# Re-spaced side work in a two-layer sequence model: scan scalings, last chunks, first loads, and attention ordered as values, queries, pool input, outputs

## The chip, the cores and the metric

One core of a Trainium2 chip runs the whole program. Times are device microseconds from one execution of the program. The engines are TensorE (PE), VectorE (DVE), ScalarE (ACT), GpSimd (POOL) and SyncE (SP), which here only issues DMAs. A smaller time is better.

## The reference

A sequence of 256 tokens with 1024 features goes through two blocks.

The first block has two layers. In each layer:

```
u = rmsnorm(h) * norm_mix_g
z, xbc, dt, g_q, g_f, g_i, g_g, m_q, m_k, m_v, m_i, m_f, m_o, gates = split(u @ w_in)
merged = gate0*(ssd(z, xbc, dt) @ w_br_ssd) + gate1*(hgrn2(...) @ w_br_hg) + gate2*(mlstm(...) @ w_br_ml)
h = h + merged @ w_out
h = h + (silu(a) * v) @ w_down      # a, v: a depthwise convolution of rmsnorm(h) @ w_up
h = h + (p @ w_ple) * sigmoid(h @ w_ple_gate)
```

The branch `ssd` ends with a root-mean-square norm over two groups of 512 channels. The second block has one layer, where mod is a linear map of silu(c), cut into six vectors:

```
h = rms_norm(x) * (1 + sc1) + sh1
q, k, v, u = split(h @ w_in)             # 4 heads, 2 maps of 64 each, values of 128; u: 4 pool groups
a_out = softmax(q0 k0) v - lam * softmax(q1 k1) v, then rms_norm per head (rotary on q and k)
p_out = (windowed means of u, minus u) @ w_pool * pool_scale
x = x + g1 * (concat(a_out, p_out) @ w_out)
x = x + g2 * moe(rms_norm(x) * (1 + sc2) + sh2)     # 32 experts, top 2 in one group
```

All arithmetic is in fp32.

## The kernel before

Features lie on the partitions in 8 chunks of 128, and the 256 tokens on the free axis. A fp32 product is three matmuls on fp32r halves (`mm3`, L484 to L486, 256 columns each): hi by hi, hi by lo and lo by hi. A weight matrix comes in units of 128x1024, in the order of a plan. For each unit SP issues the load to `w_raw` (L257), ACT casts it to `w_hi` (L296), and DVE subtracts to `w_lo` (L308), up to three units ahead of PE. `s_proj` runs one projection: two output chunks of 128 share a PSUM tile, and each takes a unit of 8 blocks, that is 24 matmuls. The first pair of a projection with `first=True` interleaves the two units (L501 to L503), so that it can follow its input chunk by chunk. `m_proj` (L528 to L530) has the weights as the moving operand, with 512 columns.

Everything else runs between these matmuls. After certain blocks of a unit (`self.hooks`, positions 2 and 6 as a rule, 3, 6 and 8 in the wide projections) PE's program calls `hook()`, which moves the next generator of `bgs` or `par` by one `yield`. A plain `yield` ends the hook, and `yield True` lets the next generator run in it too. Since each engine executes its program in the order in which it was written, a PE instruction written at a hook holds every later matmul until its input is there. `defer` and `chain` put off single functions to later hooks in the same way.

The places that the change touches are these.

- The start: `h` and four units are loaded, ACT and DVE split `h` times the first gain (`raw_add`, L703, L704) for the first projection `z0`, the squares are summed by PE (`sum_sq`, L639, a matmul with a column of ones), `rstd` (L648, L649) and `wide` (L654) give the scale for all partitions, and `norm` (L716, L719, L712) forms the normalised chunks. The matmul for the attention's lambda (L606) waits for a short chain of VectorE and ScalarE work.
- The scan's end: `ssd` sums squares of its 8 channel chunks (L639, after an add L644 on DVE), takes `rstd` and `wide`, and scales chunk by chunk (L1190, L1193, L1195). Meanwhile the hgrn2 generator does its first passes (L1262 on PE, L1242 to L1293 on ACT and DVE).
- The last chunks of `brm`, `wout` and `down`: chunks 6 and 7 leave in one pair, and their squares are summed at the end.
- The second block: eight chunks of u (L1635 on DVE, L1614 on ACT, L1615 on DVE) feed the projections u2, v2, q2 and o2. Each head is a generator `attention`: rotary matmul (L1722), scores (L1736), exponentials (L1745), transposes (L1760), product with the values (L1768), and for two groups of heads (0 to 2, and 3) a norm and transposes (L1791). `pool` is another generator (L1837). o2 (L1704 to L1706) adds eight input chunks, the pool's first, and drains the generators in while loops.
- After o2 comes the MoE, whose 192 loads of 1 MB SP issues at L275.

Of the kernel before, what the change touches and what calls it, by code (L numbers as in the profile page):

```python
# [172 lines left out]
def layout(i):  # L173
# [194 lines left out]
class Net:  # L368
    def __init__(self, ctx, tc, aps, dbg=None):
# [19 lines left out]
        for n, a, b in (("u2", 0, 4), ("v2", 4, 8), ("q2", 8, 16), ("o2", 16, 24)):  # L389
            plan += [(n, aps["win2"][u], UW) for u in range(a, b)]  # L390
# [153 lines left out]
    def setup(self):  # L544
        nc, aps, cp = self.nc, self.aps, self.cp
        self.h = self.act.tile([128, 8, T], F32, name="h")
        self.vl = {}
        self.load_vec(0)
        for c in range(0, 8, 4):
            nc.sync.dma_start(self.h[:, c:c + 4], aps["xT"][:, c:c + 4])  # L550
            self.st.load()
# [16 lines left out]
        for c in range(0, 8, 2):  # L568
            self.raw_add(0, c)
            if c < 4:  # L570
                self.st.begin()
                self.st.end()
        self.st.fill()
# [4 lines left out]
        self.flush(once=True)  # L578

    def setup2(self, lv):  # L580
# [42 lines left out]
        self.chain(lambda: None, start, lam, end)  # L623
# [9 lines left out]
    def sum_sq(self, ps, sq, first, last, add=True):  # L633

        def mm():
            for j in range(1 if add else 2):
                for tt in range(2):
                    o = j * T + tt * 128
                    self.nc.tensor.matmul(ps[:, tt:tt + 1], sq[:, o:o + 128], self.one[:, 0:1],  # L639
                                          start=first and not j and not tt, stop=last and (add or j == 1),  # L640
                                          skip_group_check=True)
        if not add:
# [1644 lines left out]
```

## Time and profile before

| | before |
|---|---|
| time, median of 3 runs (lowest to highest) | 2145.73 us (2142.51 to 2146.99) |
| profiled execution: time, span | 2140.42 us, 2138.6 us |
| mean granted TensorE clock | 0.989 |
| PE busy | 2077.2 us (97%) |
| weight load (PEld) busy | 1749.9 us (82%) |
| DVE busy | 1358.7 us (64%) |
| ACT busy | 1053.4 us (49%) |
| matmul records of L484 to L486 | 3 x 3264 |
| mean of a weight cast (ACT, L296), of a low half (DVE, L308) | 1048 ns, 1215 ns |
| mean DMA rate over the span | 224 GB/s |

Busy PE time is modelled from the matmuls' starts, so a busy PE need not run at its full rate: what a stretch could take is better read from the distance of matmul starts. Idle time of an engine that nothing waits for costs nothing.

### The profile page before, as it was taken

Reading aid. Unit: us, or ns where it says so; the run is one execution under the profiler, and the core shown is the slowest. Engines: PE = TensorE matmul, PEld = TensorE weight load, DVE = VectorE, ACT = ScalarE, POOL = GpSimd, SP = SyncE. Lnnn points to the kernel's source line nnn. Section 1 sums busy time; section 2 is a strip of 40 time slices with the busy share of each in tenths; the row PEclk is TensorE's granted clock in tenths of the full one; section 3 lists DMA queues with packets and bytes.
Section 4 is the critical chain, followed back from the end, with each engine's and each line's share of the span. In section 5 each row is a group of like instructions: output and inputs, shape, how many; then the busy total and the mean of one; then the engine's idle time right before and its main releaser. Section 6 shows DMA issues by size and latency. Waiting matters only on the chain.

```text
span 2138.6 us, 37221 instructions
## 1 busy us (share of the span) xinstructions
PE 2077.2 (97%) x15222; PEld 1749.9 (82%) x15222; DVE 1358.7 (64%) x2399; ACT 1053.4 (49%) x1686; POOL 4.2 (0%) x10
## 2 busy tenths in 40 slices
PE   8999999999999999999999999999988999999987
PEld 8988999999999999799999999999978544444323
DVE  7897787775888778887777767887676210011002
ACT  6665665664666356666666745664444211111102
POOL 0000000000000000000000000000000000000000
PEclk9999999999999999999999999999999999999999
DMA  6433444445655844344343456558545999999996
GB/s 224 151 129 128 139 148 149 141 155 174 226 194 199 312 163 175 117 138 158 138 159 119 139 202 212 183 197 307 192 138 217 394 420 420 420 420 420 421 420 261
DMA packets 106095, 482.22 MB, mean 225 GB/s; under 512 B 11712, under 2 KB 13376, under 8 KB 81344
## 3 DMA queue, kind: packets, MB, share of 16 engines
q1 hardware_dynamic: 97024, 451.41, 56.6%
q10 hardware_dynamic: 8896, 28.37, 3.8%
q8 instruction: 122, 2.00, 0.4%
q14 instruction: 53, 0.43, 0.1%
HBM read 478.69 MB, written 1.05 MB: 224 GB/s over the span
## 4 chain that ended last, share of the span: by engine, by line
PE 71%; DMA 16%; DVE 6%; ACT 5%; issue 1%; ACTq 0%; SPq 0%; DVEq 0%
PE ps_d L484 16%; PE ps_d L485 16%; PE ps_d L486 15%; DMA s<-in_moe 7%; DMA w_more<-in_moe 7%; PE ps_d L2029 3%; PE ps_b L1262 2%; PE ps_d L528 2%; PE ps_d L530 2%; PE ps_d L529 2%; PE ps_d L2055 1%; DVE w_lo L308 1%; PE ps_d L502 1%; ACT w_hi L296 1%; PE ps_b L1146 1%
## 5 line engine op out<-in xcount | busy, mean ns | idle before, releaser
L484 PE MATMUL ps_d<-s,w_hi 128*128 128x256 f32 x3264 | 934.1, 286 | 0.0
L485 PE MATMUL ps_d<-s,w_hi 128*128 128x256 f32 x3264 | 915.2, 280 | 0.0
L486 PE MATMUL ps_d<-s,w_lo 128*128 128x256 f32 x3264 | 914.9, 280 | 0.0
L296 ACT CAST w_hi<-w_raw 128x1024 fp32r<-128x1024 f32 x474 | 490.5, 1048 | 291.6 <-PE ps_d L485 209.0
L484 PEld LDWEIGHTS ps_d<-s,w_hi 128*128 128x128 f32 x3264 | 617.5, 189 | 6.6 <-issue 5.8
L485 PEld LDWEIGHTS ps_d<-s,w_hi 128*128 128x128 f32 x3264 | 617.3, 189 | 1.1 <-issue 0.5
L486 PEld LDWEIGHTS ps_d<-s,w_lo 128*128 128x128 f32 x3264 | 616.5, 189 | 0.2
L308 DVE TENSOR_TENSOR w_lo<-w_raw,w_hi 128x1024 fp32r<-128x1024 f32 x474 | 569.6, 1215 | 46.4 <-ACT w_hi L296 46.4
L2037 DVE TENSOR_TENSOR x2a<-x2a,ps_d 128x512 f32<-128x512 f32 x16 | 11.0, 688 | 177.5 <-PE ps_d L2029 177.5
L2068 DVE SCALAR_TENSOR_TENSOR s<-ps_d,m_ws,s 128x512 fp32r<-128x512 f32 (+1 forms) x34 | 24.5, 720 | 145.1 <-ACT s L2067 145.1
L2029 PE MATMUL ps_d<-s,s 128*64 128x512 f32 x424 | 98.8, 599 | 1.1 <-DMA s<-in_moe 0.9
L893 DVE SCALAR_TENSOR_TENSOR x2a<-ps_d,vl,x2a 128x255 f32<-128x255 f32 x176 | 81.0, 481 | 27.2 <-ACT x2a L886 24.1
L2029 PE MATMUL ps_d<-w_more,s 128*64 128x512 f32 x384 | 90.5, 600 | 1.8 <-DMA w_more<-in_moe 1.7
L2067 ACT ACTIVATE s<-ps_d,m_ws 128x512 fp32r<-128x512 f32 (+1 forms) x34 | 22.6, 666 | 114.1 <-PE ps_d L2055 113.0
L1262 PE MATMUL ps_b<-s,s 128*128 128x128 f32 x512 | 71.2, 284 | 5.4 <-ACT s L1284 3.5
L1262 PEld LDWEIGHTS ps_b<-s,s 128*128 128x128 f32 x512 | 65.2, 191 | 7.0 <-ACT s L1284 4.3
L2029 PEld LDWEIGHTS ps_d<-s,s 128*64 128x64 f32 x424 | 27.7, 136 | 51.6 <-issue 40.9
L1284 ACT COPY s<-s 128x512 f32<-128x512 f32 x48 | 30.5, 636 | 73.5 <-DVE s L1280 73.4
L1536 DVE SCALAR_TENSOR_TENSOR s<-s,ada_c,s 128x1024 f32<-128x1024 f32 x42 | 53.8, 1282 | 18.6 <-DMA s<-in_wada 18.4
L2029 PEld LDWEIGHTS ps_d<-w_more,s 128*64 128x64 f32 x384 | 24.8, 136 | 48.5 <-issue 37.2
L2034 ACT ACTIVATE x2a<-ps_d 128x512 f32<-128x512 f32 x16 | 9.6, 600 | 106.0 <-PE ps_d L2029 106.0
L2055 PE MATMUL ps_d<-s,x2b 128*64 128x512 f32 x248 | 57.3, 599 | 3.9 <-DMA s<-in_moe 3.9
(419 smaller groups left out, 2757.3 us busy)
## 6 DMA issues: line engine op xcount, KB each, us to landing
w_raw<-in_wl SPq DMA_DIRECT2D x448, 512.0 KB, 4.4
s<-in_moe SPq DMA_DIRECT2D x84, 1024.0 KB, 19.8
w_more<-in_moe SPq DMA_DIRECT2D x72, 1024.0 KB, 19.8
w_raw<-in_moe SPq DMA_DIRECT2D x36, 1024.0 KB, 19.9
s<-in_wada ACTq DMA_DIRECT2D x48, 512.0 KB, 5.7
w_raw<-in_win SPq DMA_DIRECT2D x24, 512.0 KB, 4.5
h<-in_xT SPq DMA_DIRECT2D x2, 512.0 KB, 6.2
w_raw<-in_wsm SPq DMA_DIRECT2D x2, 256.0 KB, 4.0
```

What stands on the lines that cost most here:

```text
L296: self.nc.scalar.copy(hi[:, :w], self.raw[i][:, :w])
L308: self.nc.vector.tensor_sub(lo[:, :w], raw[:, :w], hi[:, :w].bitcast(F32))
L484: t.matmul(out, whi, rhi, start=start, stop=False)
L485: t.matmul(out, whi, rlo, start=False, stop=False)
L486: t.matmul(out, wlo, rhi, start=False, stop=stop)
L528: t.matmul(ps[tt], a, hi[:, w], start=kc == 0, stop=False)
L529: t.matmul(ps[tt], b, hi[:, w], start=False, stop=False)
L893: nc.vector.scalar_tensor_tensor(ys[j][:, a:b], xs[j][:, a + o:b + o], w(j, k), ys[j][:, a:b], op0=OP.mult, op1=OP.add)
L1262: nc.tensor.matmul(ps[:, o:o + 128], kc[:, o:o + 128], rhs(o), start=True, stop=True)
L1536: nc.vector.scalar_tensor_tensor(acc, w, sc[:, kc:kc + 1], acc, op0=OP.mult, op1=OP.add)
L2029: t.matmul(ps[64 * j:64 * j + 64], xg[kc // 4][:, o:o + CAP], w[j][:, k2 * 512:k2 * 512 + 512], start=kc == 0, stop=kc == 7)
L2055: t.matmul(ps[64 * j:64 * j + 64], H[p][:, o:o + CAP], w[j][:, k2 * 512:k2 * 512 + 512], start=kc == 0, stop=kc == 3)
```

## The change

1. Start. The gains of the first norm come as a small load of their own (`g0`), the loads are issued in another order, both first units are cast ahead of the second half of `h`, and units 2 and 3 are cast around the norm instead of ahead of it. The lambda matmul comes some hooks later.
2. Scan. Between the steps of the norm stand more hooks, the scaling of a pair of chunks ends its hook, and the low half of a pair is formed a step later.
3. Last chunks. With `single`, `s_proj` gives each of the last two chunks a PSUM tile of its own and evacuates it alone; the sums of squares of chunks 6 and 7 go to PE apart, without DVE's add. The split of `pT` comes after the flush ahead of `wout`.
4. Second block. The projections come as v2, q2, u2, o2; the low half of a u chunk is formed one chunk later; hooks in q2 and u2 come after blocks 1, 3, 5 and 7; there are more hooks between a head's steps; the pool starts with its input; o2's chunks come as 4, 5, 0, 1, 2, 6, 7, 3 (0 to 3 are the heads); the table for the exponential is loaded ahead of q2.

The core of the diff:

```diff
+OUT2 = 4, 5, 0, 1, 2, 6, 7, 3
...
-    def s_proj(self, name, n_oc, rhs, evac, nk=8, first=False, start=0, mid=None):
+    def s_proj(self, name, n_oc, rhs, evac, nk=8, first=False, start=0, mid=None, single=False, ahead=(2, 2)):
...
+                    if one:
+                        self.defer(lambda oc=oc + j, ps=o: evac(oc, ps, 1))
+                        ps = None if j else self.ps()
...
         self.vl = {}
+        o = VO["mix_g"][0]
+        self.g0 = cp.tile([128, 8], F32, name="g0")
+        nc.scalar.dma_start(self.g0, aps["vecL"][0][:, o:o + 8])
+        nc.sync.dma_start(self.h[:, 0:4], aps["xT"][:, 0:4])
+        for _ in range(2):
+            self.st.load()
+        nc.sync.dma_start(self.h[:, 4:8], aps["xT"][:, 4:8])
         self.load_vec(0)
-        for c in range(0, 8, 4):
-            nc.sync.dma_start(self.h[:, c:c + 4], aps["xT"][:, c:c + 4])
-            self.st.load()
...
-        self.chain(lambda: None, start, lam, end)
+        none = lambda: None
+        self.chain(none, start, none, none, lam, none, end)
...
             add()
             yield True
+            yield True
             mm()
         rt = self.tmp("rt", 4)
         yield True
         self.rstd(rt, ps[:, :4], 512)
         yield True
+        yield True
...
+        def lower(c):
+            nc.vector.tensor_sub(out[1].ch(c - 1, 2), xbc.ch(c - 1, 2), out[0].ch(c - 1, 2).bitcast(F32))
         for g in range(2):
             r = pr[:, g * T:g * T + T]
-            yield True
             for c in range(4 * g, 4 * g + 4):
...
                 if c % 2:
-                    x, hi, lo = xbc.ch(c - 1, 2), out[0].ch(c - 1, 2), out[1].ch(c - 1, 2)
-                    nc.scalar.copy(hi, x)
-                    yield True
-                    nc.vector.tensor_sub(lo, x, hi.bitcast(F32))
+                    nc.scalar.copy(out[0].ch(c - 1, 2), xbc.ch(c - 1, 2))
+                    if c > 1:
+                        lower(c - 2)
+                    yield
+        lower(7)
...
-        self.split(pt[:, :512], pp[0].ch(0, 2), pp[1].ch(0, 2))
...
         self.flush()
-        self.s_proj(f"wout{l}", 8, mm, evo, first=True)
+        self.split(pt[:, :512], pp[0].ch(0, 2), pp[1].ch(0, 2))
+        self.s_proj(f"wout{l}", 8, mm, evo, first=True, single=True)
...
             nc.vector.scalar_tensor_tensor(t, self.h[:, c], self.gs1[:, c:c + 1], r2, op0=OP.mult, op1=OP.mult)
-            self.shifted(t, c, u[0].ch(c), u[1].ch(c))
+            if low:
+                low()
+            low = self.shifted(t, c, u[0].ch(c), u[1].ch(c))
+        low()
         self.rstd(r1t, self.hsum[:, :2], D)
-        self.s_proj("u2", 4, u, evu, first=True)
-        self.wide(r1, r1t)
-        self.flush()
 
         def first_out():
+            self.wide(r1, r1t)
+            yield
...
+        self.preload(AF.Exp)
...
+        self.hooks = 1, 3, 5, 7
         self.s_proj("q2", 8, u, evq)
...
+        self.s_proj("u2", 4, u, evu)
+        self.flush()
...
-        for n, c in enumerate((4, 5, 6, 7, 0, 1, 2, 3)):
-            if n == 0:
+        for n, c in enumerate(OUT2):
+            if n == 7:
                 while self.bgs:
                     self.hook()
-            elif n >= 4:
-                while any(g[0] <= c for g in self.heads()):
-                    self.hook()
+            while any(g[0] <= c for g in self.heads()) if c < 4 else self.pooled <= c - 4:
+                self.hook()
```

The first place is VectorE at the program's start. `L704` and `L718` form the low half of h times the gain, `L308` and `L309` the low half of a weight unit, `L716` and `L730` a normalised chunk, `L712` and `L726` its low half. Before:

```order
4 L704 SCALAR_TENSOR_TENSOR s_112<-h,vl,s_111 128x256 x2
5 L308 TENSOR_TENSOR w_lo<-w_raw,w_hi 128x1024
6 L704 SCALAR_TENSOR_TENSOR s_112<-h,vl,s_111 128x256 x2
7 L308 TENSOR_TENSOR w_lo<-w_raw,w_hi 128x1024
8 L704 SCALAR_TENSOR_TENSOR s_112<-h,vl,s_111 128x256 x4
9 L308 TENSOR_TENSOR w_lo<-w_raw,w_hi 128x1024 x2
10 L644 TENSOR_TENSOR sq<-sq 128x256 x2
11 L644 TENSOR_TENSOR x2a<-x2a 128x256 x2
12 L649 RECIPROCAL rt<-rt 128x2
13 L716 SCALAR_TENSOR_TENSOR u_f<-h,vl,ps_b 128x256 x2
14 L712 TENSOR_TENSOR s_235<-u_f,s_234 128x256
```

The same place in the changed kernel:

```order
4 L718 SCALAR_TENSOR_TENSOR s_114<-h,g_73,s_113 128x256 x4
5 L309 TENSOR_TENSOR w_lo<-w_raw,w_hi 128x1024 x2
6 L718 SCALAR_TENSOR_TENSOR s_114<-h,g_73,s_113 128x256 x4
7 L657 TENSOR_TENSOR sq<-sq 128x256 x2
8 L657 TENSOR_TENSOR x2a<-x2a 128x256 x2
9 L662 RECIPROCAL rt<-rt 128x2
10 L309 TENSOR_TENSOR w_lo<-w_raw,w_hi 128x1024
11 L730 SCALAR_TENSOR_TENSOR u_f<-h,vl,ps_b 128x256
12 L309 TENSOR_TENSOR w_lo<-w_raw,w_hi 128x1024
13 L730 SCALAR_TENSOR_TENSOR u_f<-h,vl,ps_b 128x256
14 L726 TENSOR_TENSOR s_230<-u_f,s_229 128x256
```

Units 2 and 3, which stood ahead of the sums, now stand on either side of the norm's first chunk.

The second place is VectorE at the scan's end in the first layer. `L644` and `L657` are the adds ahead of a sum of squares, `L649` and `L662` the norm's reciprocal, `L1190` and `L1225` the scalings, `L1195` and `L1220` their low halves, `L1280` to `L1293` and `L1316` to `L1329` the hgrn2 passes. Before:

```order
245 L644 TENSOR_TENSOR sq<-sq 128x256
246 L1250 TENSOR_TENSOR s_1955<-s_978,s_977 128x1024
247 L308 TENSOR_TENSOR w_lo<-w_raw,w_hi 128x1024
248 L649 RECIPROCAL rt<-rt 128x4
249 L308 TENSOR_TENSOR w_lo<-w_raw,w_hi 128x1024
250 L1190 SCALAR_TENSOR_TENSOR s_162<-s_162,vl,ps_b 128x256 x2
251 L1195 TENSOR_TENSOR s_1863<-s_162,s_1862 128x512
252 L1190 SCALAR_TENSOR_TENSOR s_162<-s_162,vl,ps_b 128x256 x2
253 L1280 TENSOR_TENSOR s_1867<-s_1867,s_977 128x2x256
254 L1287 TENSOR_TENSOR s_1955<-s_1955,s_977 128x2x256
```

The same place in the changed kernel:

```order
244 L657 TENSOR_TENSOR sq<-sq 128x256
245 L1286 TENSOR_TENSOR s_1952<-s_980,s_979 128x1024
246 L309 TENSOR_TENSOR w_lo<-w_raw,w_hi 128x1024
247 L657 TENSOR_TENSOR sq<-sq 128x256
248 L309 TENSOR_TENSOR w_lo<-w_raw,w_hi 128x1024
249 L1316 TENSOR_TENSOR s_1869<-s_1869,s_979 128x2x256
250 L1323 TENSOR_TENSOR s_1952<-s_1952,s_979 128x2x256
251 L1326 TENSOR_TENSOR s_979<-s_979 128x512
252 L1328 TENSOR_TENSOR s_980<-ps_b,cm 128x512
253 L1329 COPY_PREDICATED s_980<-lvm,ps_b 128x512
254 L662 RECIPROCAL rt<-rt 128x4
255 L309 TENSOR_TENSOR w_lo<-w_raw,w_hi 128x1024
```

The reciprocal and the scalings stand behind the first hgrn2 pass, not ahead of it.

The third place is VectorE at the second block's start: `L1635` and `L1672` form a chunk of u, `L1615` and `L1651` its low half, which needs ACT's high half of the same chunk. Before:

```order
1715 L1628 RECIPROCAL rt<-rt 128x2
1716 L1635 SCALAR_TENSOR_TENSOR u_f<-h,gs_17066,ps_b 128x256
1717 L1615 SCALAR_TENSOR_TENSOR s_17322<-u_f,ada_mod,s_17321 128x256
1718 L1635 SCALAR_TENSOR_TENSOR u_f<-h,gs_17066,ps_b 128x256
1719 L1615 SCALAR_TENSOR_TENSOR s_17322<-u_f,ada_mod,s_17321 128x256
```

The same place in the changed kernel:

```order
1723 L1664 RECIPROCAL rt<-rt 128x2
1724 L1672 SCALAR_TENSOR_TENSOR u_f<-h,gs_17094,ps_b 128x256 x2
1725 L1651 SCALAR_TENSOR_TENSOR s_17350<-u_f,ada_mod,s_17349 128x256
1726 L1672 SCALAR_TENSOR_TENSOR u_f<-h,gs_17094,ps_b 128x256
1727 L1651 SCALAR_TENSOR_TENSOR s_17350<-u_f,ada_mod,s_17349 128x256
```

Two chunks are formed ahead of the first low half, so that VectorE has the next chunk to form while ScalarE casts.

On TensorE, at the end of the heads, the changed kernel has 12 o2 matmuls between the last head's product with the values (`L1825`) and its transposes (the last `L1851`), and the latter end with these rows, after which 144 o2 matmuls follow:

```order
11486 L1750 MATMUL ps_b<-s_17387,w_hi 128x256
11487 L1751 MATMUL ps_b<-s_17386,w_lo 128x256
11488 L1851 MATMUL ps_b<-cm,s_17472 128x128 x2
11489 L1907 MATMUL ps_b<-s_18128,s_17072 128x256
11490 L1851 MATMUL ps_b<-cm,s_17472 128x128 x2
```

Before, 18 o2 matmuls stand between those two (`L1768`, the last `L1791`), and 120 follow.

## Rows read from the trace of the kernel before

**Rows 1.** Windows: us; busy PE, PEld, DVE, ACT, POOL; PEclk, DMA share, GB/s.

```profile
158.00:192.00 34.00, 30.23 (x246) 29.04 (x245) 28.01 (x48) 22.69 (x30) 0.00 (x0) 1.00 0.35 115
...
282.00:516.00 234.00, 233.90 (x1875) 226.07 (x1875) 174.41 (x325) 136.87 (x208) 0.74 (x1) 1.00 0.45 153
...
920.00:950.00 30.00, 27.04 (x221) 26.03 (x220) 25.89 (x46) 19.28 (x26) 0.00 (x0) 1.00 0.29 102
...
1656.00:2109.00 453.00, 438.86 (x2219) 185.18 (x2220) 52.12 (x118) 66.19 (x112) 0.00 (x0) 1.00 1.01 417
```

**Rows 2.** Waits of PE in the whole run: us in total, times, longest.

```profile
PE ps_b L639 <- DVE sq L644: 6.5, 10, 1.5
```

**Rows 3.** Timeline of PE, scan's end: start, us, instruction [idle before].

```profile
157.73 0.28 PE L484 MATMUL ps_d<-s,w_hi 128*128 128x256 f32 x1
...
160.18 0.50 PE L639 MATMUL ps_b<-one,sq 128*128 128x1 f32 x4
...
185.92 1.16 PE L1262 MATMUL ps_b<-s,s 128*128 128x128 f32 x8 [1.50 <-ACT s L1284]
...
191.02 0.36 PE L484 MATMUL ps_d<-s,w_hi 128*128 128x256 f32 x1
```

**Rows 4.** Timeline of PE where the second hgrn2 pass group starts, first layer.

```profile
277.88 1.05 PE L1262 MATMUL ps_b<-s,s 128*128 128x128 f32 x8
...
281.10 0.42 PE L484 MATMUL ps_d<-s,w_hi 128*128 128x256 f32 x1
```

**Rows 5.** Timeline of ACT in the same stretch.

```profile
276.20 1.28 ACT L797 ACT_TABLE_LOAD   x1
277.49 0.60 ACT L797 ACTIVATE s<-ps_d 128x512 f32<-128x512 f32 x1
```

**Rows 6.** Timeline of PE in the first 36 us.

```profile
12.45 0.38 PE L503 MATMUL ps_d<-s,w_lo 128*128 128x256 f32 x1 [0.76 <-DVE w_lo L308]
...
35.01 0.38 PE L606 MATMUL ps_b<-lam,cm 128*128 128x2 f32 x2 [1.88 <-DVE lam L602]
```

**Rows 7.** Timeline of DVE in the first layer's first norm.

```profile
22.77 0.48 DVE L716 SCALAR_TENSOR_TENSOR u_f<-h,vl,ps_b 128x256 f32<-128x256 f32 x1
...
23.62 0.48 DVE L716 SCALAR_TENSOR_TENSOR u_f<-h,vl,ps_b 128x256 f32<-128x256 f32 x1
```

**Rows 8.** Timeline of ACT ahead of wout in the first layer.

```profile
526.13 0.62 ACT L536 CAST s<-s 128x512 fp32r<-128x512 f32 x1 [3.08 <-DMA s<-in_pT]
```

**Rows 9.** PE by line, second block, 1545.8 to 1653: busy, mean ns, idle.

```profile
L1736 PE MATMUL ps_b<-s 64*128 64x256 f32 x32 | 5.3, 451 | 3.2 <-DVE s L1729 2.3 <-ACT w_hi L296 0.9
...
L1760 PE MATMUL ps_b<-cm,x2b 128*128 128x128 f32 x16 | 3.6, 313 | 4.3 <-DVE x2b L1755 4.3
L1837 PE MATMUL ps_b<-u_f,s 128*128 128x256 f32 x8 | 2.5, 398 | 1.7 <-DVE u_f L1832 1.7
L1791 PE MATMUL ps_b<-cm,s 128*128 128x128 f32 x8 | 1.6, 286 | 2.4 <-DVE s L1786 2.4
```

**Rows 10.** Windows of 5 us in the second block, same columns.

```profile
1545.00:1550.00 5.00, 4.83 (x22) 4.25 (x22) 2.91 (x7) 1.85 (x4) 0.00 (x0) 0.53 0.01 3
...
1600.00:1605.00 5.00, 4.75 (x25) 4.15 (x26) 4.97 (x11) 0.59 (x1) 0.00 (x0) 0.67 0.00 0
...
1625.00:1630.00 5.00, 4.68 (x30) 4.13 (x28) 3.44 (x11) 3.35 (x13) 0.00 (x0) 0.78 0.00 0
```

**Rows 11.** Timeline of DVE over the eight chunks of u.

```profile
1545.86 0.48 DVE L1615 SCALAR_TENSOR_TENSOR s<-u_f,ada_mod,s 128x256 fp32r<-128x256 f32 x1 [0.58 <-ACT s L1614]
...
1556.05 0.48 DVE L1615 SCALAR_TENSOR_TENSOR s<-u_f,ada_mod,s 128x256 fp32r<-128x256 f32 x1 [0.58 <-ACT s L1614]
```

**Rows 12.** Timeline of PE from u2's first matmul to its second pair.

```profile
1545.87 0.58 PE L501 MATMUL ps_d<-s,w_hi 128*128 128x256 f32 x1 [0.17 <-ACT s L1614]
...
1557.28 0.28 PE L484 MATMUL ps_d<-s,w_hi 128*128 128x256 f32 x1
```

**Rows 13.** Timeline of SP's load issues around the end of o2.

```profile
1642.67 13.73 SPq L275 DMA_DIRECT2D w_more<-in_moe  x6
```

More of the change, by code (lines that the diff above doesn't have):

```diff
@@ L493, in s_proj @@
             if first and oc == start:
-                w = [self.st.get(name, ahead=2) for _ in range(2)]
+                w = [self.st.get(name, ahead=k) for k in ahead]
                 for kc in range(nk):
@@ L569, in setup @@
             self.raw_add(0, c)
[L570 to L573, printed above, removed]
+            if c == 2:
+                for _ in range(2):
+                    self.st.begin()
+                    self.st.end()
+        self.st.pump()
         for c in range(0, 8, 2):
@@ L631, in vec, with sum_sq @@
         return self.vl[self.l][:, o:o + n]
-    def sum_sq(self, ps, sq, first, last, add=True):
+    def sum_sq(self, ps, sq, first, last, w=2):
         def mm():
[L636 to L642, printed above, removed]
+            for tt in range(2):
+                self.nc.tensor.matmul(ps[:, tt:tt + 1], sq[:, tt * 128:tt * 128 + 128], self.one[:, 0:1],
+                                      start=first and not tt, stop=last, skip_group_check=True)
+        if w == 1:
             return [mm]
@@ L720, in norm @@
             late.append((lo.ch(c), u, hi.ch(c)))
+            if c == 0 and mid:
+                mid()
         lower()
@@ L752, in layer, with parts @@
         if RAW[l]:
-            self.s_proj(f"z{l}", 2, self.hg, evr, first=True, mid=lambda: self.flush(once=True))
+            self.s_proj(f"z{l}", 2, self.hg, evr, first=True, mid=lambda: self.flush(once=True),
+                        ahead=(2, 2) if l else (0, -1))
             last_ = self.later.pop()
-        u = self.norm(self.vec("mix_g", 0, 8), self.h_rstd())
+        r = self.h_rstd()
+        def parts():
+            self.st.begin()
+            self.st.end()
+        if l == 0:
+            self.st.end()
+        u = self.norm(self.vec("mix_g", 0, 8), r, None if l else parts)
         if RAW[l]:
@@ L967, in last_add @@
         ps = self.hsum2[:, :2]
-        self.defer(lambda: self.chain(*self.sum_sq(ps, sq, c == 0, c == 6, c < 6)))
+        if c < 6:
+            steps = self.sum_sq(ps, sq, c == 0, False)
+        else:
+            parts = [self.sum_sq(ps, sq[:, j * T:], False, j == 1, 1)[0] for j in range(2)]
+            steps = [lambda: [f() for f in parts]]
+        self.defer(lambda: self.chain(*steps))
     def h_rstd(self):
@@ L1839, in pool @@
             yield
-        out()
+        yield from out()
         yield
```

135 lines of the change are left out of this document (87 added, 48 removed).

## The prediction

> **What bounds the kernel now.** I read the windows by stage first. In a plain stretch of a layer PE is busy without a gap (233.90 of 234 us) while DVE and ACT have a quarter or more of their time free [rows 1], so there nothing but fewer or faster matmuls would help, and the change touches neither. At full clock the starts lie 0.117 us apart: 21 matmuls from 157.73 to 160.18 [rows 3]. Two kinds of stretches are otherwise. At the scan's end PE is busy 30.23 of 34.0 us in the first layer and 27.04 of 30.0 in the second [rows 1], and in the second block there are waits for DVE at every step of a head [rows 9]. After 1656 the DMA engines are full (share 1.01, 417 GB/s) [rows 1], and that stretch is the MoE's loads. Does time saved ahead of it reach the end? SP's load of `w_more` at 1642.67 holds its issue for 13.73 us while o2 runs [rows 13]; these loads reuse buffers that PE's work frees, so I let the saving pass one to one, and price the other case as a rival.
>
> **The start.** PE gets its first full pair of units at 12.45, after a wait of 0.76 for a low half [rows 6]. Casting both units ahead of the second half of h should bring this forward by about one cast's wait, 1.2 us. The lambda matmul waits 1.88 us for its chain [rows 6]; it now comes 24 matmuls later, and 24 x 0.117 = 2.8 us covers it. Against this, units 2 and 3 now stand around the first chunk of the norm on DVE and ACT: chunks come 0.85 us apart [rows 7], and a cast and a low half put in between delay chunk 1 and all behind it by about 1 us, and the next unit's low half by as much again. PE follows chunk by chunk, so this counts. Sum 1.2 + 1.9 - 2.1 = 1.0 us; from -1 (nothing gained at the head) to 2.5 (half of the delay covered).
>
> **The scan's end.** From the first sum at 160.18 to 191.02 there are 30.84 us [rows 3]. The work in it is 157 matmuls of 256 columns (18.3 us), 16 records of sums, 8 of `wide` and 40 of L1262, together about 7 us: 25 us. So 5.6 us are lost, 3.77 as idle time [rows 1], the rest in slow starts after each wait. The largest single wait, 1.50 us ahead of an L1262 [rows 3], comes because the scalings and the hgrn2 pass take DVE in the same hooks. In the changed order the sums stand 24 matmuls (2.8 us) apart instead of 15 to 18, and the scalings come one pair in a hook behind the first hgrn2 pass. I walked the new order with the old durations and found two waits left: about 1.4 us at the third sum, whose add now stands behind six hgrn2 instructions on DVE, and 0.8 at one L1262. That saves 3.5 us in this layer and 3.0 in the other, whose idle time is 2.96 [rows 1]: 6.5 us. Below, nothing; above, 9. The later hgrn2 passes shift by about 30 matmuls and still have over 100 behind them.
>
> **Where the second group of passes starts.** From 277.88 to 281.10, 16 records of L1262 take 3.22 us [rows 4], of which some 2 are work by the distance of those at the scan's end. ACT is late there: it loads a table at 276.20 for 1.28 us, and the next activation starts at 277.49 [rows 5]. In the new order this activation stands beside others of its table and that load is gone. I take 1.0 us a layer, 2.0 in all (0 to 2.5). The Trainium skill ("ScalarE: Activation LUTs", What ACT_TABLE_LOAD costs) gives 1.28 us for the load and as much again for a drain, 2.66 together. The trace agrees on the load and shows no drain in front of or behind it, 276.20 + 1.28 being 277.48. By the page the two layers could return up to 4 us, and the sum below would be 2 us larger; I keep the row.
>
> **The last chunks.** PE waits ten times, 6.5 us in all, for DVE's add ahead of a sum of squares [rows 2]; most of it lies at the scan's ends and at another norm that doesn't change. The single chunks remove an add and start the last sum one chunk earlier: 0.5 us for each `wout`. ACT waits 3.08 us for the load of pT with the evacuation of `brm` queued behind the split [rows 8]; moved behind the flush it holds nobody up, which returns about 1.2 us in the first layer. Sum 2.2 us (1 to 3). The price is one more evacuation for each tail on DVE, which is not the limit there.
>
> **The second block.** All matmuls from 1545.87 to 1653 take 107 us. By the program there are 480 of 256 columns (56 us), 48 of 512 (11.3 at twice the distance) and the heads' own, about 15.5: 83 us. So 24 are lost. Named waits are 3.2 + 4.3 + 1.7 + 2.4 = 11.6 [rows 9]; another 5.8 go in the first pair of u2, 48 matmuls in 11.41 us [rows 12] instead of 5.6; the rest goes at the lower clock, granted 0.53, 0.67 and 0.78 in three windows [rows 10].
> Three things happen. (a) The chunks of u: DVE forms a chunk, ACT casts it, DVE idles 0.58 us for the cast [rows 11], and eight chunks take (1556.05 - 1545.86)/7 = 1.46 us each. With the low half a chunk later the chain is that of the first norm, 0.85 us [rows 7], so the last is there about 4.3 us sooner. v2 goes first now, and its matmuls are long, so it will run behind the chunks in part at the lower clock, and `wide` for r1 stands after 15 of its 48 matmuls and waits for a reciprocal that is queued behind all chunks. I take 2.5 us (0.5 to 3.2). (b) The heads have 24 hooks of 6 matmuls (0.7 us each) instead of 11 of 12, and u2 as cover behind them. The waits at L1736, L1760 and L1837 should mostly go. What is late next: the rotary product's evacuation stands on ACT behind a weight cast that waits for PE, about 0.6 us a head, 2.4 in all. (c) At the end the last head has 12 matmuls between its values and its transposes where 18 stood, and a wait of 2.4 us stays as about 2. With some 4 us of slow starts and clock I count 11 of 24 left: a gain of 13 us for the block (7 to 17).
>
> **Sum.** 1.0 + 6.5 + 2.0 + 2.2 + 13 = 24.7 us. The profiled execution took 2140.42; the median of the runs is 5.3 above it. 2140.42 - 24.7 = 2115.7, and with the 5.3 it is 2121 us. The parts' lower ends sum to about 7.5 us, the upper to 34. All lower ends together are unlikely; the forecast's own range is 2112 to 2128.
>
> **Rivals.** A change within 0.2% (4.3 us) can't be told from none.
> 1. The heads trade one wait for another. More, shorter hooks put PE instructions nearer to their inputs: six matmuls are 0.7 us, while a step through DVE or ACT with a weight cast of 1.05 to 1.2 us ahead of it is longer. Then the block gains only 4: 15.7 in all, 2130 us. For it: DVE was busy 4.97 of 5 us at 1600 [rows 10]. Against it: a step now has several hooks.
> 2. The scan's end is DVE's. DVE is busy 28.01 of 34 us there [rows 1], so spacing alone would change nothing: 18.2 us in all, 2127.5. Against it: DVE does nearly as much in the stretches without a gap, and its units may run three ahead. With the first rival as well, 9.2 us: 2136.5.
> 3. The MoE's loads don't start earlier with o2. They fill the DMA engines from 1656 on; if half of the block's gain is lost, 18.2 us are left, 2127.5. Against it: the loads wait for buffers that o2 frees [rows 13].
> 4. Slower: the lower clock holds through the second block. At half clock a 256-column matmul costs 0.117 us more. To eat the 24.7 us and 4.3 more, 29/0.117 = 248 of the block's 480 must run so beyond those that do already; with 300 the time is 2121 + 35 = 2156 us. It is granted 0.53 in the first window of the block and falls again after heavy waits [rows 10], and hooks every 0.7 us could bring many such waits. The Trainium skill ("TensorE: Matmul & The Clock Gate", Part 1) calls the lower rate the default, which activity lifts; by it waits that only move would keep the rate down, and that is this rival. Against it: the clock is 1.00 through the scan's end with all its gaps [rows 1].
>
> **How the numbers follow.** The forecast has a chance of 0.55; rival 1 alone 0.15; 2 alone 0.10; 1 and 2 together 0.06; 3 0.07; 4 0.07. All but rival 4 end faster by over 0.2%, 0.93; I take 0.05 off for several of the small terms failing in them, 0.04 of it to within 0.2%, 0.01 to slower. Of rival 4, 0.02 ends within 0.2% and 0.05 slower. So faster 0.88, within 0.2% 0.06, slower 0.06. The range 2108 to 2136 leaves out rival 4, rivals 1 and 2 together, and the forecast's far end, 0.18.
>
> **What would show it.** Right: sums at the scan's end waiting once at most, no table load ahead of the second pass group, chunks of u 0.85 us apart, no wait over 1 us in q2, and o2's end 25 us earlier with the MoE's stretch of equal length. Wrong: L667 in v2 or L1851 at the heads' end waiting several us, PEclk near 0.5 over more than two windows, or a longer MoE stretch.

## The result and the profile after

The changed kernel takes 2123.64 us, median of 5 runs (2119.73 to 2128.01), against 2144.46 of the kernel before in the same comparison (2142.51 to 2146.99). The ratio is 0.990, with a 95% interval of 0.9885 to 0.9916: 20.8 us or 1.0% faster. The prediction was 2121, range 2108 to 2136. A second comparison (e5 below) gave 0.9919 (0.9903 to 0.9934).

The profiled execution of the changed kernel is the slowest of its five (2128.01), and that of before (2140.42) is faster than all five of its kernel here, so the two profiles lie only 12.4 us apart. Read side by side they show the waits, but not what the change is worth in all: single executions of one kernel differ by more than the missing 8 us, as the last section tells.

The scan's ends first. These windows have the columns of [rows 1]; the first two hold the scan's end of either layer in the changed kernel:

```profile
150.00:185.00 35.00, 34.02 (x284) 32.69 (x281) 29.51 (x54) 23.65 (x32) 0.00 (x0) 1.00 0.41 139
...
910.00:945.00 35.00, 35.00 (x299) 34.94 (x299) 30.66 (x51) 26.12 (x34) 0.00 (x0) 1.00 0.41 139
```

PE is busy 34.02 of 35 and 35.00 of 35 us, where it had 30.23 of 34 and 27.04 of 30 [rows 1]. In the new order the hgrn2 pass goes on a little behind either window, and there one of its products (L1298, L1262 before) waits once more, 0.78 us at 193.81 and 0.82 at 946.42. The waits that were left in the first layer, as PE's waits between 150 and 560 us (us in total, times, longest):

```profile
PE ps_b L653 <- DVE sq L657: 2.2, 4, 1.0
PE ps_d L503 <- ACT s L733: 1.0, 1, 1.0
PE ps_b L1298 <- ACT s L1320: 0.8, 1, 0.8
```

Of the four waits at a sum of squares (L653) one lies at the scan's end, the third sum's, with 1.0 us at 172.16; the other three come later, with 1.2 us together. PE's wait at the start of the second pass group, which was for ACT's copy behind a table load [rows 4, 5], is no longer in the list.

At the start PE now waits for the second chunk of the norm. Timeline of PE:

```profile
8.61 0.38 PE L503 MATMUL ps_d<-s,w_hi 128*128 128x256 f32 x1 [1.20 <-ACT w_hi L297]
...
11.23 0.58 PE L505 MATMUL ps_d<-s,w_lo 128*128 128x256 f32 x1 [0.36 <-DVE w_lo L309]
...
26.44 0.38 PE L504 MATMUL ps_d<-s,w_hi 128*128 128x256 f32 x1 [1.98 <-DVE s L726]
```

The second unit's low half is there at 11.23 instead of 12.45 [rows 6] (the first unit's comes as before, at 9.86 against 9.89), and the second chunk's low half (L726) costs 1.98 us at 26.44. The lambda matmul waits no more.

In the second block, the chunks of u on DVE:

```profile
1538.92 0.87 DVE L1672 SCALAR_TENSOR_TENSOR u_f<-h,gs,ps_b 128x256 f32<-128x256 f32 x2 [0.80 <-PE ps_b L667]
...
1540.50 0.48 DVE L1672 SCALAR_TENSOR_TENSOR u_f<-h,gs,ps_b 128x256 f32<-128x256 f32 x1
...
1541.41 0.48 DVE L1672 SCALAR_TENSOR_TENSOR u_f<-h,gs,ps_b 128x256 f32<-128x256 f32 x1
...
1546.12 0.48 DVE L1651 SCALAR_TENSOR_TENSOR s<-u_f,ada_mod,s 128x256 fp32r<-128x256 f32 x1 [0.18 <-ACT s L1650]
```

A chunk is formed every 0.91 us. DVE idles 0.18 us at the first and the last low half, where it idled 0.58 at each of the eight, and the last low half starts 7.2 us after the first chunk (1538.92), before 11.25 us (1544.80 to 1556.05). PE by line for the block (records, busy, mean ns, then idle time and what ended it):

```profile
L1749 PE MATMUL ps_d<-s,w_hi 128*128 128x256 f32 x48 | 14.9, 310 | 3.5 <-ACT s L1875 3.5
...
L1825 PE MATMUL ps_b<-s,x 128*128 128x128 f32 x32 | 5.2, 314 | 1.1 <-ACT x L1819 1.1
...
L1785 PE MATMUL ps_b<-s 64*128 64x256 f32 x32 | 4.5, 402 | 0.0
L1767 PE MATMUL ps_b<-s,s 128*128 128x512 f32 x8 | 4.5, 644 | 1.0 <-ACT s L1704 0.9
...
L1907 PE MATMUL ps_b<-s,s 128*128 128x256 f32 x8 | 3.0, 456 | 0.0
...
L1815 PE MATMUL ps_b<-cm,x2b 128*128 128x128 f32 x16 | 2.4, 272 | 0.0
...
L1851 PE MATMUL ps_b<-cm,s 128*128 128x128 f32 x8 | 1.7, 293 | 1.4 <-DVE s L1844 1.4
```

The waits at the scores (L1785), the transposes (L1815) and the pool's product (L1907) are gone, 9.2 us in [rows 9]. About 4 us are new in o2, 3.5 of them in one wait (L1749) and 0.9 in another (L1750), and 1.1 and 1.0 at the product with the values (L1825) and the rotary product (L1767). The place in o2, on PE:

```profile
1606.42 0.39 PE L1750 MATMUL ps_d<-s,w_hi 128*128 128x256 f32 x1 [0.85 <-DVE s L1877]
...
1607.12 0.59 PE L1907 MATMUL ps_b<-s,s 128*128 128x256 f32 x2
...
1611.14 0.53 PE L1851 MATMUL ps_b<-cm,s 128*128 128x128 f32 x2 [0.89 <-DVE s L1844]
1615.16 0.58 PE L1749 MATMUL ps_d<-s,w_hi 128*128 128x256 f32 x1 [3.50 <-ACT s L1875]
```

and on ACT and on DVE:

```profile
1608.94 1.28 ACT L1840 ACT_TABLE_LOAD   x1
1610.24 0.30 ACT L1840 ACTIVATE g_rs<-g_ss,eps 128x6 f32<-128x6 f32 x1
1614.70 0.41 ACT L1875 CAST s<-u_f 128x256 fp32r<-128x256 f32 x1 [4.17 <-DVE u_f L1874]
```

```profile
1610.57 0.19 DVE L1841 RECIPROCAL g_rs<-g_rs 128x6 f32<-128x6 f32 x1 [2.73 <-ACT g_rs L1840]
1610.80 1.26 DVE L1844 TENSOR_SCALAR s<-s,g_rs 128x128 f32<-128x128 f32 x6
1611.97 0.43 DVE L1892 TENSOR_TENSOR s<-s 128x271 f32<-128x271 f32 x1
...
1614.19 0.48 DVE L1874 TENSOR_SCALAR u_f<-ps_b,vg 128x256 f32<-128x256 f32 x1
```

o2's first chunk is the pool's first, whose low half (L1877) comes 0.85 us late at 1606.42. Its second chunk is the pool's second, which ACT casts at 1614.70 (L1875). Its product on PE (L1907) was issued at 1607.12, but DVE scales the result only at 1614.19 (L1874): that instruction stands behind the norm of heads 0 to 2 (L1841, L1844), which waits on ACT for a table load of 1.28 us (1608.94) behind a weight cast, and behind the window sums of the pool's third chunk, which begin at 1611.97 (L1892). Behind this wait the clock is low, as it is at the block's start and in the MoE's router behind o2:

```profile
1540.00:1545.00 5.00, 5.00 (x14) 3.92 (x14) 4.82 (x11) 2.71 (x6) 0.00 (x0) 0.50 0.01 3
...
1615.00:1620.00 5.00, 4.84 (x21) 4.67 (x22) 4.25 (x9) 1.94 (x4) 0.00 (x0) 0.50 0.00 0
...
1645.00:1650.00 5.00, 5.00 (x26) 5.00 (x25) 0.65 (x4) 0.41 (x2) 0.00 (x0) 0.50 1.01 419
```

Behind o2's last matmul the rest of the program takes 485.60 us, before 485.87. SP's issue of `w_more` comes at 1630.65 instead of 1642.67 [rows 13], 12.0 us earlier, in an execution that ends 12.4 us earlier:

```profile
1607.90 22.70 SPq L276 DMA_DIRECT2D w_raw<-in_moe  x3
1630.65 12.43 SPq L276 DMA_DIRECT2D w_more<-in_moe  x6
...
1671.14 4.90 SPq L276 DMA_DIRECT2D w_raw<-in_moe  x3
```

Two things cancel in this. The next loads to `w_raw` are issued at 1671.14 where the kernel before has this row,

```profile
1681.36 4.90 SPq L275 DMA_DIRECT2D w_raw<-in_moe  x3
```

so only 10.2 us earlier: about 2 us of the lead are lost on the way, in the stretch where the clock is low in the router. Then, while the DMA engines are full, they move 424 GB/s instead of 420. In turn before, the changed kernel, e1 and e4 (below):

```profile
1760.00:2060.00 300.00, 294.31 (x1469) 120.65 (x1467) 29.00 (x53) 40.62 (x68) 0.00 (x0) 1.00 1.01 420
1760.00:2060.00 300.00, 294.72 (x1471) 121.31 (x1469) 28.25 (x52) 40.44 (x68) 0.00 (x0) 1.00 1.01 424
1760.00:2060.00 300.00, 295.15 (x1476) 121.74 (x1474) 28.30 (x52) 41.18 (x69) 0.00 (x0) 1.00 1.01 424
1760.00:2060.00 300.00, 293.78 (x1466) 120.80 (x1464) 27.86 (x52) 40.49 (x68) 0.00 (x0) 1.00 1.01 420
```

All seven profiles of kernels with the edits of the start (the first of the changed kernel, e1, e5, e6, e7, e10, e11) have 424 here, and all six without them 420. The MoE's 192 loads, 201 MB, would take 475 us at the one rate and 479 at the other, so by this estimate the start's edits return some 4 us in a stage that they don't touch.

### The profile page after: what moved, and what is told of

It is laid out like the page before. It is cut to its first block, busy times and chain, and to the rows that moved or that the text cites. A ratio compares the mean times of both kernels' runs of the same rounds, so it can differ in the third digit from the quotient of the medians.

```text
span 2126.2 us, 37231 instructions
## 1 busy us (share of the span) xinstructions
PE 2079.0 (98%) x15222; PEld 1757.1 (83%) x15222; DVE 1357.7 (64%) x2411; ACT 1044.3 (49%) x1685; POOL 4.3 (0%) x10
## 4 chain that ended last, share of the span: by engine, by line
PE 81%; DMA 8%; DVE 6%; ACT 3%; issue 1%; ACTq 0%; SPq 0%; DVEq 0%
PE ps_d L485 16%; PE ps_d L486 16%; PE ps_d L487 16%; PE ps_d L2099 8%; PE ps_d L2125 4%; DMA w_more<-in_moe 4%; PE ps_b L1298 3%; DMA s<-in_moe 3%; PE ps_d L537 2%; PE ps_d L539 2%; PE ps_d L538 2%; PE ps_b L2046 1%; DVE w_lo L309 1%; PE ps_b L2147 1%; ACT w_hi L297 1%
## 5 line engine op out<-in xcount | busy, mean ns | idle before, releaser
L309 DVE TENSOR_TENSOR w_lo<-w_raw,w_hi 128x1024 fp32r<-128x1024 f32 x474 | 569.9, 1216 | 45.2 <-ACT w_hi L297 45.1
L1298 PE MATMUL ps_b<-s,s 128*128 128x128 f32 x512 | 71.0, 284 | 1.7 <-ACT s L1320 1.6
L1298 PEld LDWEIGHTS ps_b<-s,s 128*128 128x128 f32 x512 | 65.4, 191 | 3.5 <-ACT s L1320 2.3
L537 PE MATMUL ps_d<-w_hi,s 128*128 128x512 f32 x144 | 61.0, 424 | 0.0
```

The lines of the kernel that those rows point to most:

```text
L309: self.nc.vector.tensor_sub(lo[:, :w], raw[:, :w], hi[:, :w].bitcast(F32))
L537: t.matmul(ps[tt], a, hi[:, w], start=kc == 0, stop=False)
L1298: nc.tensor.matmul(ps[:, o:o + 128], kc[:, o:o + 128], rhs(o), start=True, stop=True)
```

## Experiments

Each was timed in 5 rounds against the kernel before. Ratios are to the kernel before, with 95% intervals. Us are the ratio's distance from 1 times about 2142. "The block" with a length in us is the second block in a profile, from the last product matmul ahead of it to o2's last (a product matmul is one with a weight unit): 114.4 us before and 108.1 in the changed kernel.

**e1, the start alone.** The hunks of the diff that concern the first loads, `g0`, the casts around the norm and the lambda chain.

```diff
-            self.st.load()
+        self.g0 = cp.tile([128, 8], F32, name="g0")
...
+        u = self.norm(self.vec("mix_g", 0, 8), r, None if l else parts)
```

Expected: 

> The kernel before with the edits of the start and the lambda matmul alone. Theory A (the sum of the prediction): 1.0 us faster, -1 to 2.5. Theory B (the changed kernel's profile, where PE stands 3.3 us later than before at 130 us): about 3 us slower, with a wait of about 2 us for the low half of the second chunk (L726 there) and the granted clock of the first 45 us below the 0.89 of before.

Measured: 2138.13 us, ratio 0.9990 (0.9977 to 1.0004): 2 us faster, not clear of nothing. Theory B's wait is there (2.4 us), its 3 us of loss are not: in this execution PE was 3.6 us ahead of before at its 144th product matmul, in the changed kernel's own 1.5 behind, with the same instructions. What follows o2 took 482.6 us in e1's profile, at the higher DMA rate shown above, and 485.9 to 486.6 in those of before, e2 and e3.

**e2, the scan alone.** The hunk of `ssd`.

```diff
             add()
             yield True
+            yield True
             mm()
```

Expected: 

> The kernel before with the scan's hooks alone. Theory A: 6.5 us from the two scan ends and 2.0 from the second pass group, 8.5 us faster. Theory B (PE's lead in the changed kernel, matmul by matmul): 3.1 and 4.5 us at the scan ends and about 2 a layer behind them, of which over half is given back within the next 100 us, so 6 to 9 us faster. A third, that the scan's end is VectorE's: no change.

Measured: 2132.9 us, ratio 0.9963 (0.9948 to 0.9978): 7.9 us faster (4.7 to 11.1). A and B hold, the third theory falls. Counted matmul by matmul between the same two products, PE gains 4.3 us in the first layer (from its 720th to its 3000th) and 3.6 in the second (6100th to 8200th).

**e3, the last chunks alone.** `single`, the sums apart and the later split of pT.

```diff
-        self.s_proj(f"wout{l}", 8, mm, evo, first=True)
+        self.split(pt[:, :512], pp[0].ch(0, 2), pp[1].ch(0, 2))
+        self.s_proj(f"wout{l}", 8, mm, evo, first=True, single=True)
```

Expected: 

> The kernel before with the single last chunks, the sums apart and the later split alone. Theory A: 2.2 us faster (1 to 3). Theory B (PE's lead in the changed kernel): 0.5 in the first layer, 0.8 in the second, and 1.6 at the first layer's end, about 3 us faster.

Measured: 2139.35 us, ratio 0.9999 (0.9984 to 1.0015): nothing that the timing resolves (3.4 us faster to 3.2 slower; theory A's 2.2 and theory B's 3 both lie inside). In its profile PE gains 1.37 us at the later split, in the changed kernel's too.

**e4, the second block alone.** All hunks of `block2`, `attention` and `pool`, with the plan.

```diff
-        for n, c in enumerate((4, 5, 6, 7, 0, 1, 2, 3)):
+        for n, c in enumerate(OUT2):
```

Expected: 

> The kernel before with the second block's edits alone. Theory A: 13 us faster (7 to 17). Theory B (PE's lead grows from 5.9 to 12.1 us over the block in the profiled execution, with a wait of 3.5 us in o2 and about 6 us of half clock behind it): 6 us faster in an execution that has both, and if the rest of the difference between the medians (20.8) and the profiles (12.4) is in this block, up to 14.

Measured: 2134.05 us, ratio 0.9969 (0.9952 to 0.9985): 6.6 us faster (3.2 to 10.3). Theory A's 13 is outside, its lower end of 7 is not. The profile has the same 3.5 us wait in o2, and the block takes 108.3 us.

The four parts sum to 16.9 us by ratios, a little under the 17.4 and the 21.4 of the two comparisons of the whole change, and well within what the parts' intervals leave open.

**e5, the changed kernel again.** No edit.

Expected: 

> The changed kernel again, with a second profile. If the part of the difference between the medians and the profiles is the clock granted in each execution, the waits in this profile are those of the first one and the granted clock in the first 30 us and around 1540 and 1615 differs; the time lies in 2118 to 2128 us.

Measured: 2126.08 us, ratio 0.9919, inside the expected 2118 to 2128. The granted clock differs as expected, 0.83 and 1.00 from 10 to 20 and 20 to 30 us where the first profile has 0.50 and 0.67. Its waits in the second block are those of the first profile (3.5, 1.3, 1.1, 0.8), with one more, 1.6 us at L667, where v2 had a higher clock (0.98 in 1540 to 1545, against 0.50) and caught up with the chunks.

**e6, u2 ahead of q2.** In the changed kernel.

```diff
-OUT2 = 4, 5, 0, 1, 2, 6, 7, 3
+OUT2 = 4, 5, 6, 7, 0, 1, 2, 3
...
-        self.s_proj("u2", 4, u, evu)
+        self.s_proj("u2", 4, u, evu)
+        self.s_proj("q2", 8, u, evq)
```

Expected: 

> The changed kernel with the projections as v2, u2, q2, o2 and o2's chunks as 4, 5, 6, 7, 0, 1, 2, 3, so that the pool is done during q2. Theory A (the 3.5 us wait in o2 is the pool's second chunk, whose adds stand on DVE behind the first heads' norm): that wait and the lower clock behind it go, 4 to 6 us faster than the changed kernel. Rival (u2's matmuls were the cover for the last heads): waits at L1815, L1825 and L1851 grow by as much, and the time is the same or longer.

Measured: 2123.01 us, ratio 0.9893 (0.9879 to 0.9908), against the 0.9919 (0.9903 to 0.9934) of the changed kernel in the same comparison: 5.6 us by the ratios, 3.1 by the medians, with intervals that overlap a little. Against the first comparison of the changed kernel (0.990) it is 1.5 us. Faster than the changed kernel is likely by this, not shown. PE's waits in the block (us in total, times, longest):

```profile
PE ps_b L1851 <- DVE s L1844: 4.3, 2, 2.6
PE ps_b L1767 <- ACT s L1704: 4.2, 2, 3.7
```

The wait for the pool's second chunk is gone, as theory A says, and others have come: 1.6 and 2.6 us at the heads' last transposes (L1851), which the rival named, and 3.7 at the first head's rotary product (L1767), which it did not. The latter's input is copied on ACT behind the pool's third chunk. These two lines alone wait 8.5 us, where the changed kernel's waits in the block sum to about 8, and the block takes 107.9 us, hardly less than its 108.1.

**e7, the low half of u in its own step again.** In the changed kernel.

```diff
-            if low:
-                low()
-            low = self.shifted(t, c, u[0].ch(c), u[1].ch(c))
-        low()
+            self.shifted(t, c, u[0].ch(c), u[1].ch(c))()
```

Expected: 

> The changed kernel with the low half of each chunk of u again in the step of the chunk itself. Theory A: chunks 1.46 us apart again, 2.5 us slower than the changed kernel (0.5 to 3.2). Rival (v2 behind the chunks runs at the lower clock in either case, and 48 long matmuls take about as long as the chunks): no difference.

Measured: 2130.51 us, ratio 0.9933 (0.9916 to 0.9950), 3.0 us slower than the changed kernel by the ratios and 4.4 by the medians; the intervals overlap, so the time alone doesn't exclude the rival. In the profile PE waits 4.8 us at L667, in the middle of v2, for the reciprocal behind the chunks:

```profile
PE ps_b L667 <- DVE rt L662: 4.8, 1, 4.8
```

That is 3.2 to 4.5 us more than in the two profiles of the changed kernel, and the block takes 114.4 us, 6 more than in those two. So theory A holds, with a loss at its upper end or above.

**e8, order without spacing.** The kernel before with the second block's order, pool and chunks; heads and hooks as before.

Expected: 

> The kernel before with the second block's order, the pool's steps and the chunks of u as in the changed kernel, and with the heads' generator and the hooks (after blocks 2 and 6) as before. The whole block's change alone was worth 6.6 us (3.2 to 10.3). Theory A (the spacing of the heads' steps takes their waits away): this gives 2 to 4 us, the chunks' share, and waits at L1745 and L1769 as long as those of before. Rival (the order alone, with u2 as cover behind the heads, does it): 6 us or more.

Measured: 2136.88 us, ratio 0.9967 (0.9954 to 0.9980): 7.1 us faster (4.3 to 9.9), as much as the whole block's change in e4. By time this is the rival's figure. In its profile the block takes 111.4 us, 2 to 6 less than the 113.6 to 117.0 of the four profiles with the block of before: near theory A's 2 to 4. PE's waits:

```profile
PE ps_d L1713 <- ACT s L1821: 5.5, 2, 4.6
PE ps_b L1745 <- DVE s L1738: 3.9, 3, 1.3
PE ps_b L1769 <- DVE x2b L1764: 1.2, 4, 0.3
```

The scores still wait 3.9 us (2.3 + 0.9 before [rows 9]), as theory A says, the transposes 1.2 (4.3 before), and o2 waits 5.5 for the pool's chunks, 4.6 of it in front of the first.

**e9, spacing without order.** The kernel before with the heads' steps and hooks alone.

```diff
+        self.hooks = 1, 3, 5, 7
         self.s_proj("q2", 8, u, evq)
```

Expected: 

> The kernel before with the extra steps and hooks of the heads alone (hooks after blocks 1, 3, 5 and 7 in q2 and behind it); the order u2, v2, q2, o2, the pool and the chunks of u stay as before. Theory A (the spacing of the heads' steps takes their waits away, as the prediction has it): 4 to 8 us faster, the waits at L1741 and L1771 (scores and transposes) under 1 us in all. Rival (what the order gives, the spacing doesn't add to): 0 to 2 us, waits moved to the last heads' transposes L1807.

Measured: 2136.7 us, ratio 0.9968 (0.9954 to 0.9982): 6.9 us faster (3.9 to 9.9), and the block takes 110.8 us. Theory A. The scores and transposes don't wait at all; what is left:

```profile
PE ps_b L1807 <- DVE s L1800: 4.3, 2, 2.6
PE ps_b L1856 <- DVE u_f L1851: 3.7, 2, 2.0
```

Order with the chunks of u 7.1, spacing 6.9, both (e4) 6.6: by these times the two don't add up. By the block's length they nearly do: 111.4 and 110.8 stand against 113.6 to 117.0, on average 3.6 and 4.2 us shorter, and 108.3 for both is 6.7 shorter. The times have intervals of 3 us either way, the lengths are of one execution each, so whether the two may be added stays open. Only the transposes' waits are shortened by either alone. The stall in o2 comes with the order: 4.6 us in e8, 3.5 in e4, none in e9.

**e10, both new stalls of e6 taken away.** The first head's rotary product four hooks later, and while o2 waits for heads 0 to 2, head 3 stands still.

```diff
+            if upto < 3 and g.gi_frame.f_locals["hd"] == 3:
+                continue
...
-        yield
+        for _ in range(1 if hd else 5):
+            yield
```

Expected: 

> The kernel with u2 ahead of q2 and two more edits: the first head's rotary product comes four hooks later, and while PE's program waits for heads 0 to 2 it doesn't advance head 3, whose last steps then lie among the o2 matmuls of chunks 0 to 2. Theory A: the waits of 3.7 us at L1770 and of 2.6 us at the last L1854 go, with the lower clock behind them, 4 to 6 us faster than with u2 first alone, 26 to 30 us faster than before. Rival (VectorE and ScalarE can't do the heads' work in less, and a wait appears elsewhere): 0 to 2 us.

Measured: 2119.39 us, ratio 0.9879 (0.9864 to 0.9894): 25.9 us faster than before, at the lower end of theory A's 26 to 30. The block takes 106.2 us, 1.7 less than in e6, and the longest wait in it is 2.1 us:

```profile
PE ps_b L1854 <- DVE s L1847: 2.1, 1, 2.1
PE ps_d L1751 <- ACT s L1859: 1.3, 2, 1.0
```

Against e6 (0.9893, another comparison) it is 3 us, and the intervals overlap: neither theory A's 4 to 6 nor the rival's 0 to 2 is shown by the time. Against the changed kernel it is clear of the comparison in e5 (0.9903 to 0.9934) and overlaps the first one (0.9885 to 0.9916).

**e11, the same with units 2 and 3 ahead of the norm.**

```diff
-        self.st.pump()
+        self.st.fill()
```

Expected: 

> The same with units 2 and 3 cast and split ahead of the first norm again, as before, the rest of the new start kept. Theory A (units around the norm delay its chunks): the wait of 2.0 us for the second chunk's low half (L726 in the changed kernel) goes, and PE stands 1 to 2 us earlier at its 240th matmul. Rival (the units are missed at the first sums of squares instead): no difference.

Measured: 2120.76 us, ratio 0.9894 (0.9879 to 0.9909), not told apart from e10. PE stands 3.0 us earlier than in e10 at its 240th product matmul, at 48.6 us, but with a higher granted clock (0.79 and 0.87 against 0.50 and 0.67 from 10 to 30 us); e5, which has the units around the norm and 0.83 and 1.00 there, is at that matmul at 48.0. The 2.0 us for L726 are gone and 1.9 us stand at the first sums of squares, behind the two casts: the rival. PE's waits in the first 150 us, of e11 and then of e10, where L506 waits for the low half L728 (L504 and L726 in the changed kernel):

```profile
PE ps_b L654 <- DVE sq L658: 1.9, 1, 1.9
```

```profile
PE ps_d L506 <- DVE s L728: 2.0, 1, 2.0
```

## Why the prediction was right, and which terms were not

The time, 2123.6, lies 2.6 us from the forecast and inside its own range of 2112 to 2128. The gain is 20.8 us, 17.4 in the second comparison, where the sum had 24.7. One term was right, one was about twice what came, two are not seen, and some us came from a place that had no term; so that the total came this near is in part luck.

The times of the single parts are known to some 3 us. The thirteen profiles tell some stages better, if the same product matmuls are compared in each, counted from the program's start. Lengths in us, lowest to highest:

| stage, by product matmuls | profiles without the edit concerned | with it |
|---|---|---|
| start, to the 240th | 48.0 to 52.7 (6) | 46.6 to 51.7 (6) |
| first layer's scan, 720th to 3000th | 374.7 to 374.9 (6) | 370.4 to 370.6 (7) |
| between the scans, with the first layer's last chunks, 3000th to 6100th | 413.8 to 421.2 (6) | 415.4 to 420.3 (7) |
| second layer's scan, 6100th to 8200th | 340.5 to 340.7 (6) | 337.0 to 337.2 (7) |
| second block (before, e1, e2, e3; after, e4, e5) | 113.6 to 117.0 (4) | 108.1 to 108.4 (3) |

By terms:

- **The start**, 1.0 (-1 to 2.5): 2 us measured, -1 to 5. Its parts came as worked out: the second unit's low half 1.2 us earlier, no wait for lambda, and the delay of the second chunk, seen as one wait of 2.0. But the 240th matmul comes no sooner with it than without it. What e1 gained is seen behind o2, where the DMA engines move 424 GB/s instead of 420, and the prediction had no term for that.
- **The scan's ends and the second pass group**, 6.5 + 2.0: 7.9 measured (4.7 to 11.1), and 4.3 + 3.5 in the profiles, the same in all seven that have the edit. The two waits that were left were foreseen at 1.4 and 0.8 us; they are 0.98 and 0.78 in the first layer. The rival that VectorE is the bound there is refuted by e2. Of three table loads on ACT between 267 and 278 us two are left (269.22 and 276.75), and 73 of 79 in the whole run. The 2.66 us that the Trainium skill ("ScalarE: Activation LUTs", What ACT_TABLE_LOAD costs) gives for a table load found no support: the load shown above begins where the cast ahead of it ends (1608.93), and its activation follows 1.30 us after its start (1608.94 to 1610.24, the two rows of ACT).
- **The last chunks**, 2.2: between -3 and 3.4, not resolved by time. The later split gives 1.4 where 1.2 were predicted, but the stage that holds it is no shorter in the seven profiles with the edit; the rest isn't settled.
- **The second block**, 13 (7 to 17): 6.6 measured (3.2 to 10.3), 5 to 9 by the profiles, the term that was mis-sized. (a), the chunks of u, held: a pitch of 0.91 instead of 0.85, and 3 to 4 us by e7's times, 6 by its profile, for the 2.5 taken. (b) held as to the waits at scores, transposes and pool, 9.2 us of them gone. The step that failed is the count of what is left, "11 of 24". From its first matmul to o2's end the block takes 100.8 us, so by the same count (83 us of work) about 18 are left. Of these some 8 are named waits where the prediction had 4.4. It had the rotary product's evacuation at 2.4 (0.9 came) and under (c) the last head's transposes at 2 (1.4 came), and nothing for what o2 waits for first, the pool's chunks: 0.9 us in front of the low half of the first, 3.5 in front of the second, and then about 5 us at half clock. I had moved the pool behind q2 without asking which of its chunks o2 needs first and what stands ahead of it on VectorE: the heads' norm, which waits for a table, and the pool's own third chunk. The other 10 us, where it had 6.6, are slow starts and the lower clock. e6 takes the pool's wait away, but others come and the block is no shorter. In e10, where the longest wait is 2.1 us, it takes 106.2, on average 8.7 less than the block of before: so the stall in o2 is a part of what is missing from 13, not all of it.
- **The MoE**: in this pair of profiles the time passed on one to one, but only since two effects cancel: 2 us of the lead are lost behind o2 and about as much or more comes back with the DMA rate. In e4 and e8, which have the new order and the old rate, what follows o2 takes 489.2 and 489.5 us where before, e2 and e3 have 485.9 to 486.6. So rival 3 holds in small, 3 us of the block's gain, not 6.5. Rival 4 came in a small form too: three windows of 5 us at 0.50, at the block's start, in o2 and in the MoE's router, where the lowest two before were 0.53 and 0.67 [rows 10]. Its sign, more than two windows near 0.5, came true, and it cost some us, not 29. At the lower clock the starts lie 0.213 us apart (1616.21 to 1616.42 on PE), so a matmul costs 0.097 us more there, not the 0.117 that rival 4 took, and 5 us at that clock cost about 2.3.

Rival 1, that the heads trade one wait for another, is what happened to half of the block's gain: it gave 6.6 where the forecast had 13 and the rival 4. With 6.6 for the block the forecast's own sum would be 18.3 us and 2127.4. The lower ends of the parts sum to 7 us, not 7.5, which changes nothing else.

## What to carry to other kernels

When work is moved behind other work as cover, look at the first thing that the next stage needs, and at each in-order queue ahead of it: a wait that is taken away in three places can come back in one if a chunk of another generator stands behind a chain there. And where single executions differ by several microseconds, two profiles tell which waits exist, not what they are worth. Compare a stage between the same two matmuls in every profile at hand: the scan's gain repeats to 0.2 us so, while the totals scatter by ten. Look also at the stages that the change leaves alone: here the MoE's loads got faster without an edit to them.

## What the runs showed of the hardware

I had not expected how far executions of one program differ. The kernel before took 2134.14 to 2147.67 us in 35 runs. The first 30 us are the same instructions in before and in the kernels of e2, e3 and e4, and the granted clock in windows of 10 us there was not. In turn before, e2 and e3:

```profile
10.00:20.00 10.00, 8.16 (x49) 7.55 (x50) 7.21 (x14) 7.85 (x13) 0.00 (x0) 0.81 1.03 410
20.00:30.00 10.00, 10.00 (x72) 9.72 (x71) 8.21 (x18) 5.31 (x11) 0.00 (x0) 0.85 0.20 70
```

```profile
10.00:20.00 10.00, 8.32 (x38) 7.86 (x38) 7.05 (x13) 7.56 (x12) 0.00 (x0) 0.59 1.03 406
20.00:30.00 10.00, 10.00 (x64) 9.92 (x64) 6.00 (x16) 3.10 (x8) 0.00 (x0) 0.73 0.13 52
```

```profile
10.00:20.00 10.00, 8.61 (x48) 8.04 (x49) 7.33 (x14) 7.83 (x13) 0.00 (x0) 0.66 1.03 410
20.00:30.00 10.00, 10.00 (x77) 9.25 (x76) 8.60 (x18) 5.67 (x12) 0.00 (x0) 1.00 0.21 70
```

With 0.59 and 0.73 (e2) PE stands 2.5 us behind before at its 240th product matmul, with 0.66 and 1.00 (e3) 1.9 us ahead; e4 had 0.80 and 0.86 and stands level. In the kernels with the new start the same windows had about 0.50 and 0.67 three times (the changed kernel's first profile, e6, e10) and at least 0.83 in both three times (e1, e5, e7). So a stall at the start costs its own length and then some microseconds, more or fewer, at the lower of the two clock levels, and a profile shows one draw. The second block, with its many stalls, scatters alike: that of before took 114.4, 115.0, 117.0 and 113.6 us in before, e1, e2 and e3. What decides it isn't settled by these runs.

Not every small difference is scatter. Behind o2 the DMA rate belongs to the kernel, not to the execution: it is 424 GB/s between 1760 and 2060 us in all seven profiles of kernels with the edits of the start, and 420 in all six without them. e11 casts its units ahead of the norm as before and still has 424, so it isn't the casts around the norm; which of the other edits does it, the new load and tile of the gains, the order of the loads and of the first casts, or the later lambda matmul, no run tells.
